# Attention stage of a decoder layer: one run of transpositions for each slot, with the compressed ones directly ahead of it and the preceding slot's first values ahead of both

## The chip, the cores and the metric

The kernel runs on one core of a Trainium2 chip. The metric is the time of one execution on the device, in microseconds (us); the median of three runs is given. One further execution was recorded by the hardware profiler, and all rows below come from it. The engines are TensorE (PE, with its weight loads listed apart as PEld), VectorE (DVE), ScalarE (ACT), GpSimd (POOL) and SyncE (SP), which issues DMAs.

## What is computed

One layer of a decoder trunk over 512 positions of width 2048, in float32. The part that matters here is the sparse attention: 16 heads of 64 in 4 groups, three branches (compressed, selected blocks, sliding window), each with its own keys and values, mixed by gates. Cut to that part, the reference is:

```python
q, kv, g_logits, z_a, uv, z_b, merge_logits = jnp.split(h @ w_in, SPLIT_IDX, axis=-1)
# compressed branch: 31 overlapping blocks of 32 positions
p_c = jax.nn.softmax(jnp.where(vc_mask, sc - slopes * dc, NEG), axis=-1) * vc_mask
o_c = jnp.einsum('bgrqn,bngd->bqgrd', p_c, vc)
# selected blocks and window: scores, ALiBi, softmax, values
p_s = jax.nn.softmax(ss);  o_s = jnp.einsum('bgrqnk,bgqnkd->bqgrd', p_s, vs)
p_w = jax.nn.softmax(sw);  o_w = jnp.einsum('bgrqk,bkgd->bqgrd', p_w, vwb)
o_a = (g0 * o_c + g1 * o_s + g2 * o_w) * silu(z_a)
```

Around it stand the input projection, a chunked gating branch, two up-projections, the output projection, a per-layer embedding under a gate and a final norm. With 512 positions there are 8 blocks of 64 and up to 16 may be selected, so the selected branch sees every causal position, as the window does.

## The kernel before

All matrix products with the large weights are done in two float32 parts, a high and a low one (`hi` and `lo`; three matmuls for each product). The halves are made by `split`: ScalarE casts the high part (`high`, line 200), VectorE subtracts to get the low one (`low`, line 206). With `later=True` the subtraction is put on the list `deferred`, and the next `flush` issues it.

Projections are a stream of small units of work, made by a generator. `fill(n)` takes the next n units from it; in the attention stage a unit is three matmuls of 512 columns (lines 588 to 590, tiles `ps_q` and `ps_za`), and their weight halves are made on ScalarE and VectorE two pieces ahead. These units are the filler between the pieces of attention, which are short and depend on each other.

The attention stage (trace: about 213 to 462 us) goes over 48 slots, six for each of eight feature tiles `ft` of two heads. A slot is a query tile `i` of 128 positions with one branch or both: `(ft, 3, (0,))`, `(ft, 3, (1,))`, `(ft, 2, (0,))`, `(ft, 2, (1,))`, `(ft, 1, (0, 1))`, `(ft, 0, (0, 1))`; `j` counts them from 0 to 5. The loop has 51 periods, and works on several slots at once: in period s it makes the `scores` of slot s (TensorE into `ps_s`, then a VectorE reduction, line 1611), the `exponentials` of s (ScalarE, line 1620), `weigh` of s - 1 (VectorE, line 1636), the transpositions of s - 2 (`transpose_probs`, line 1661) and the `values` of s - 3 (lines 1680 and 1681).

The transpositions of a slot come in one or two blocks of up to four. Each block fills one PSUM bank `ps_t` (there are two, of the kind "t"); ScalarE casts it to `pth`, VectorE makes `ptl` from both (three buffers of each), and `values` reads these two. For every even `ft` the compressed branch adds steps of its own: `cmp_softmax` at j = 1 (four transpositions into a bank of the kind "s", line 1733, a copy, a shift in three VectorE steps, lines 1743 to 1745), `cmp_weigh` at j = 3 (VectorE lines 1753 to 1755, then GpSimd lines 1756 and 1757), `cmp_transpose` at j = 4 (line 1763, then a copy `pc`, two casts and two subtractions). The banks of the kind "s" are shared by `ps_s` and `ps_c`, and there are two of them.

The order of a period is written out as the list `events`. After each event that uses TensorE some filler is taken by a running `credit`; `off_pe` events take none, and no event is followed by a `flush` of its own: the `flush` stands ahead of the next event that uses TensorE. In the list, the first block of transpositions stands ahead of the exponentials, the first block of values behind them, then `cmp_softmax` or `cmp_transpose`, then the second block of transpositions and the second block of values. All engines take their instructions in the order in which the program issues them.

Of the kernel before, what the change touches and what calls it, by code (L numbers as in the profile page):

```python
# [117 lines left out]
def kernel(ctx: ExitStack, tc: tile.TileContext, x, p, norm_g, w_in,  # L118
# [15 lines left out]
    def bank(kind, name):  # L134
        return psum.tile([P, 512], F32, tag=kind, name=name)
# [56 lines left out]
    def flush():  # L192
        todo = list(deferred)
        deferred.clear()
        for f in todo:
            f()
# [14 lines left out]
    def split(hi, lo, src, scale=None, later=False):  # L211

        high(hi, src, scale)
        if later:
            deferred.append(lambda: low(hi, lo, src, scale))
        else:
            low(hi, lo, src, scale)
# [120 lines left out]
    def load_next():  # L338
        while state["loads"] < len(loads):
            b = before[state["loads"]]  # L340
            tag = loads[state["loads"]][0]
            if tag in SPOTS and not spots.get(tag):
                return
            if b is not None and last_sub[b] >= state["low"]:
                return
            if tag not in SPOTS + ("raw",) and {"b11": "free"}.get(tag, "pool") not in quad:
                if not quad.get("b12"):
                    return
            load_to(state["loads"])
# [283 lines left out]
    def fill(n):  # L633
        for _ in range(n):
            next(run, None)
# [281 lines left out]
    phase_b_units = 16 * 14  # L917
# [721 lines left out]
    def blocks(s):  # L1639
        ft, i, br = slots[s]  # L1640
        if i == 0:
            return [[(0, 0), (1, 0)]]
        res = []
        for j in range(len(br)):
            ks = list(range(i + 1))
            for a in range(0, len(ks), 2):
                res.append([(j, k) for k in ks[a:a + 2]])
        return res
# [3 lines left out]
    def transpose_probs(s, bi):  # L1652
        ft, i, br = slots[s]
        n = (i + 1) * P
        pts = prob[s][0]
        bl = blocks(s)[bi]
        b = bank("t", "ps_t")
        for e, (j, k) in enumerate(bl):
            for hh in range(2):
                c = j * n + k * P  # L1660
                nc.tensor.transpose(b[:, (2 * e + hh) * P:(2 * e + hh + 1) * P], pts[hh][:, c:c + P], ident)  # L1661
        w = 256 * len(bl)
        hi = att.tile([P, S], F32R, tag="pth", name="pth", bufs=3)
        lo = att.tile([P, S], F32R, tag="ptl", name="ptl", bufs=3)
        split(hi[:, :w], lo[:, :w], b[:, :w], later=True)
        moved[s, bi] = (hi, lo)

    def values(s, bi):
        ft, i, br = slots[s]
        g = ft // 2  # L1670
        bl = blocks(s)
        hi, lo = moved.pop((s, bi))
        if i % 2 == 1 and br[0] == 0 and bi == 0:
            obank[ft, i // 2] = bank("o", "ps_o")
        o = obank[ft, i // 2][:, (i % 2) * 256:(i % 2) * 256 + 256]
        for e, (j, k) in enumerate(bl[bi]):
            w = vt[:, br[j], k, g]
            first = br[j] == 0 and bi == 0 and e == 0
            last = br[j] == 1 and bi == len(bl) - 1 and e == len(bl[bi]) - 1
            nc.tensor.matmul(o, w, hi[:, e * 256:e * 256 + 256], start=first, stop=False)  # L1680
            nc.tensor.matmul(o, w, lo[:, e * 256:e * 256 + 256], start=False, stop=last)
        if i % 2 == 0 and br[-1] == 1 and bi == len(bl) - 1:
            fold(ft, i // 2)

    def fold(ft, hf):
        o = obank.pop((ft, hf)).rearrange("p (i h q) -> p i h q", i=2, h=2)
        dst = o32[:, ft, 256 * hf:256 * hf + 256]
        gated = (ft, 256 * hf) in half_done
        tf = att.tile([P, S], F32, tag="zt", name="fold")[:, :256] if gated else dst
        half_done.add((ft, 256 * hf))  # L1690
        t = tf.rearrange("p (i q) -> p i q", i=2)
        nc.scalar.copy(t[0:64], o[64:128, :, 0])
        nc.scalar.copy(t[64:128], o[0:64, :, 1])

        def add():
            nc.vector.tensor_tensor(out=t[0:64], in0=t[0:64], in1=o[0:64, :, 0], op=ALU.add)
            nc.vector.tensor_tensor(out=t[64:128], in0=t[64:128], in1=o[64:128, :, 1], op=ALU.add)
            nc.gpsimd.tensor_tensor(out=tf, in0=tf, in1=oc_t[ft][:, 256 * hf:256 * hf + 256], op=ALU.add)
            if gated:
                nc.gpsimd.tensor_tensor(out=dst, in0=dst, in1=tf, op=ALU.mult)  # L1700
                o32_complete(ft, 1)
        deferred.append(add)
# [87 lines left out]
        f(0)  # L1790
    fill(6)
    n = len(slots)
    credit, per_period = 0.0, (phase_b_units - 19) / (n + 3)

    def load_sums(k):
        for p, o in (("5", ob_h), ("6", ob_l)):
            nc.gpsimd.dma_start(o[:, k], hsum_dram[p][:, k])

    for s in range(n + 3):
        events = []  # L1800
        state["slot"] = slots[s][0] if s < n else None, s % 6
        if s == n:
            quad["free"] = True
            load_next()
        if s < n:
            ft, j = slots[s][0], s % 6
            events.append((scores, s))
        if 1 <= s <= n:
            events.append((weigh, s - 1))
        if s < n and ft % 2 == 0 and j == 3:  # L1810
            events.append((cmp_weigh, ft // 2))
        tq = [(transpose_probs, s - 2, bi) for bi in range(len(blocks(s - 2)))] if 2 <= s <= n + 1 else []
        vq = [(values, s - 3, bi) for bi in range(len(blocks(s - 3)))] if s >= 3 else []
        more = s < n and ft % 2 == 1 and ft < 7 and j == 5
        if more:
            events.append((cmp_scores, (ft + 1) // 2, 0))
        events += tq[:1]
        if s < n:
            events.append((exponentials, s))
        events += vq[:1]  # L1820
        if more:
            events.append((cmp_scores, (ft + 1) // 2, 1))
        if s < n:
            if ft % 2 == 1 and ft < 7 and j == 3:
                events.append((cmp_keys, (ft + 1) // 2))
            if ft % 2 == 0 and (ft > 0 and j == 1 or j == 4):
                events.append(({1: cmp_softmax, 4: cmp_transpose}[j], ft // 2))
        if s in (0, 43):
            state.update(rate=0 if s else 1.41, due=0, late=0.6)
        if s in (26, 38):  # L1830
            load_sums(slice(0, 4) if s == 26 else slice(4, 6))
        events += tq[1:]
        if s < n and j == 5 - 2 * (ft % 2):
            events.append((cmp_values, ft))
        events += vq[1:]
        share = per_period / sum(e[0] not in off_pe for e in events)
        for at, e in enumerate(events):
            if e[0] not in off_pe:
                flush()
            e[0](*e[1:])  # L1840
            if e[0] not in off_pe:
                credit += share
                ahead = at + 1 < len(events) and events[at + 1][0] is cmp_transpose
                credit -= len(lent)
                lent.clear()
                units = max(int(credit) + ahead, e[0] is scores)
                fill(units)
                credit -= units
        if s % 6 == 5:
            for f in held:  # L1850
                f()
            held.clear()
# [584 lines left out]
    n = 0  # L2437
# [35 lines left out]
```

## Time and profile before

| | us |
|---|---|
| median of 3 runs | 1500.58 (1500.29 to 1500.77) |
| the profiled execution, whole | 1499.92 |
| its span, first to last instruction | 1498.2 |
| TensorE busy | 1488.6 (99%) |
| VectorE busy | 1238.9 (83%) |
| ScalarE busy | 879.3 (59%) |
| GpSimd busy | 434.6 (29%) |
| granted TensorE clock, mean | 0.999 |

An engine's busy time is a mean over stages. The starts of successive matmuls tell more than their durations, since matmuls overlap: a 512-column matmul is listed with 0.39 us, and the next one starts 0.23 us behind it. A wait shows as a start that is late against this step.

### The profile page before, as it was taken

To read this page: it belongs to the slowest core of one execution; us is meant where nothing else is said; L and a number is where in the kernel's file an instruction comes from. 1 tells how busy PE (TensorE), PEld (TensorE's weight loads), DVE (VectorE), ACT (ScalarE), POOL (GpSimd) and SP (SyncE) were. 2 spreads that over 40 slices of the span, in tenths; PEclk is the share of its full clock that TensorE was granted. 3 is DMA by queue.
4 is the path that set the end of the run, shared out by engine and by line. 5 is a ranking of instruction groups with operands and counts; after the bars stand their busy time and mean duration, and the time that the engine had idled before them with its cause. 6 is when DMAs were issued, how large, how long until landed. Compare 5 with 4: busy or idle time off the path is not lost.

```text
span 1498.2 us, 20471 instructions
## 1 busy us (share of the span) xinstructions
PE 1488.6 (99%) x7166; PEld 1245.0 (83%) x7166; DVE 1238.9 (83%) x1846; ACT 879.3 (59%) x1500; POOL 434.6 (29%) x650
## 2 busy tenths in 40 slices
PE   9999999999999999999999999999999999999998
PEld 8988888888888888888888888888888888888886
DVE  7887879999997888978888879797877985778877
ACT  7554467777765555555655555555556555655564
POOL 1331044333432242433444323221211223101220
PEclk9999999999999999999999999999999999999999
DMA  9789579889886795978798957596698999989693
GB/s 325 212 246 298 145 167 218 166 200 257 199 201 233 236 298 138 297 162 271 188 283 221 283 135 245 192 311 253 259 356 273 291 239 312 305 264 313 158 305 141
DMA packets 187063, 359.41 MB, mean 240 GB/s; under 512 B 15432, under 2 KB 73424, under 8 KB 184016
## 3 DMA queue, kind: packets, MB, share of 16 engines
q0 software_dynamic: 73472, 181.00, 46.1%
q1 hardware_dynamic: 113344, 176.84, 35.9%
q8 instruction: 56, 0.92, 0.2%
q14 instruction: 47, 0.39, 0.1%
q10 hardware_dynamic: 144, 0.26, 0.0%
HBM read 298.81 MB, written 114.82 MB: 276 GB/s over the span
## 4 chain that ended last, share of the span: by engine, by line
PE 92%; DVE 2%; issue 2%; DMA 1%; ACT 1%; POOL 1%; POOLq 0%; DVEq 0%; ACTq 0%
PE ps_m L561 6%; PE ps_m L562 6%; PE ps_m L563 6%; PE ps_wo L562 3%; PE ps_wo L563 3%; PE ps_wo L561 3%; PE ps_pg L500 3%; PE ps_pg L502 3%; PE ps_pg L501 3%; PE ps_t L1661 2%; PE ps_za L588 2%; PE ps_za L589 2%; PE ps_za L590 2%; PE ps_kv L561 2%; PE ps_u L561 2%
## 5 line engine op out<-in xcount | busy, mean ns | idle before, releaser
L206 DVE TENSOR_TENSOR ls<-b,hs 128x1024 fp32r<-128x1024 f32 x223 | 272.5, 1223 | 110.3 <-ACT hs L200 109.1
L200 ACT CAST hs<-b 128x1024 fp32r<-128x1024 f32 x223 | 234.7, 1053 | 203.2 <-PE ps_m L563 47.1
L200 ACT CAST hs<-raw 128x1024 fp32r<-128x1024 f32 x139 | 146.5, 1055 | 134.6 <-issue 34.3
L206 DVE TENSOR_TENSOR ls<-raw,hs 128x1024 fp32r<-128x1024 f32 x139 | 169.9, 1222 | 54.9 <-ACT hs L200 54.6
L464 POOL COPY pad_r<-pad_r 128x1 f32<-128x1 f32 x55 | 50.6, 920 | 211.7 <-ACT pad_r L463 211.6
L561 PE MATMUL ps_m<-hs,act_h 128*128 128x512 f32 x256 | 100.2, 391 | 0.0
L562 PE MATMUL ps_m<-ls,act_h 128*128 128x512 f32 x256 | 99.8, 390 | 0.0
L563 PE MATMUL ps_m<-hs,act_l 128*128 128x512 f32 x256 | 99.7, 389 | 0.0
L376 DVE TENSOR_TENSOR b<-raw,b 128x1024 f32<-128x1024 f32 x68 | 82.8, 1218 | 1.5 <-DMA raw<-in_w_in_dram 1.4
L376 DVE TENSOR_TENSOR b<-b,b 128x1024 f32<-128x1024 f32 x64 | 78.0, 1218 | 0.0
L200 ACT CAST pth<-ps_t 128x512 fp32r<-128x512 f32 (+1 forms) x88 | 47.6, 544 | 46.0 <-PE ps_t L1661 45.5
L1620 ACT ACTIVATE prob<-prob,st 128x512 f32<-128x512 f32 (+3 forms) x128 | 70.7, 556 | 5.3 <-DVE st L1611 5.2
L206 DVE TENSOR_TENSOR lo<-raw,hi 128x512 fp32r<-128x512 f32 (+1 forms) x96 | 63.2, 663 | 6.3 <-ACT hi L200 5.5
L200 ACT CAST hi<-raw 128x512 fp32r<-128x512 f32 (+1 forms) x96 | 56.1, 591 | 19.0 <-PE ps_vcg L603 5.3
L206 DVE TENSOR_TENSOR ptl<-ps_t,pth 128x512 fp32r<-128x512 f32 (+1 forms) x88 | 55.5, 636 | 8.0 <-ACT pth L200 7.3
L1611 DVE CUSTOM_DVE_ANT_0 prob<-ps_s,b 128x512 f32<-128x512 f32 (+3 forms) x128 | 56.1, 485 | 3.9 <-PE ps_s L1602 3.6
L562 PEld LDWEIGHTS ps_m<-ls,act_h 128*128 128x128 f32 x256 | 48.1, 188 | 10.3 <-DVE ls L206 0.5
L563 PEld LDWEIGHTS ps_m<-hs,act_l 128*128 128x128 f32 x256 | 48.1, 188 | 10.2
L561 PEld LDWEIGHTS ps_m<-hs,act_h 128*128 128x128 f32 x256 | 48.1, 188 | 9.8
L588 PE MATMUL ps_za<-act_h,hi 128*128 128x512 f32 x128 | 53.9, 421 | 0.0
L1636 DVE TENSOR_SCALAR prob<-prob,st,gates 128x512 f32<-128x512 f32 (+3 forms) x128 | 51.9, 458 | 1.8
L588 PE MATMUL ps_q<-act_h,hi 128*128 128x512 f32 x128 | 52.2, 407 | 0.0
(768 smaller groups left out, 4598.1 us busy)
## 6 DMA issues: line engine op xcount, KB each, us to landing
raw<-in_w_in_dram SPq DMA_DIRECT2D x112, 512.0 KB, 5.3
b<-in_w_in_dram SPq DMA_DIRECT2D x58, 512.0 KB, 6.5
o<-in_w_out_dram POOLq DMA_DIRECT2D x48, 512.0 KB, 7.8
t<-in_w_up_b_dram POOLq DMA_DIRECT2D x24, 512.0 KB, 9.6
b<-o SPq DMA_DIRECT2D x18, 512.0 KB, 7.3
o<-o POOLq DMA_DIRECT2D x16, 512.0 KB, 6.3
act_l<-gate POOLq DMA_DIRECT2D x8, 1024.0 KB, 12.7
g<-in_w_ple_gate_dram POOLq DMA_DIRECT2D x16, 512.0 KB, 7.6
```

Of the source, the lines that this page charges most:

```text
L200: nc.scalar.copy(hi, src)
L206: nc.vector.tensor_tensor(out=lo, in0=src, in1=hi.bitcast(F32), op=ALU.subtract)
L376: nc.vector.tensor_tensor(out=b[o], in0=b[x], in1=b[y], op=ALU.subtract)
L464: nc.gpsimd.tensor_copy(steps[:, 16 + i:17 + i], steps[:, i:i + 1])
L500: nc.tensor.matmul(o, ah, hi[:, i], start=begins, stop=False, skip_group_check=go)
L561: nc.tensor.matmul(o, ah, wh, start=st, stop=False, skip_group_check=go)
L562: nc.tensor.matmul(o, ah, wl, start=False, stop=False, skip_group_check=go)
L563: nc.tensor.matmul(o, al, wh, start=False, stop=sp, skip_group_check=go)
L588: nc.tensor.matmul(ps, hi[:, j], ah, start=st, stop=False)
L1611: nc.vector.tensor_tensor_reduce(out=pt[:, j * n:j * n + n], in0=o[:, j], in1=b0[:, 512 - n:], scale=-SLOPE[h], scalar=3.0e38, op0=ALU.add ...
L1620: nc.scalar.activation(sl, sl, AF.Exp, bias=st[:, 0, j, hh:hh + 1], scale=-1.0, accum_out=st[:, 1, j, hh:hh + 1])
L1636: nc.vector.tensor_scalar(out=sl, in0=sl, scalar1=st[:, 1, j, hh:hh + 1], scalar2=gates[:, i, gate:gate + 1], op0=ALU.mult, op1=ALU.mult)
```

## The change

The loop's list of events is put in another order. All blocks of transpositions of a slot are one event now (`transpose_all`), behind the first block of values of the preceding slot. `cmp_softmax` and `cmp_transpose` stand between these two, and no filler is taken behind them, so their four transpositions come directly ahead of the slot's own. The exponentials follow behind the transpositions. The count of units that the filler holds back goes from 19 to 20.

```diff
+    def transpose_all(s):
+        for bi in range(len(blocks(s))):
+            transpose_probs(s, bi)
+
...
-    credit, per_period = 0.0, (phase_b_units - 19) / (n + 3)
+    credit, per_period = 0.0, (phase_b_units - 20) / (n + 3)
...
-        tq = [(transpose_probs, s - 2, bi) for bi in range(len(blocks(s - 2)))] if 2 <= s <= n + 1 else []
+        tq = [(transpose_all, s - 2)] if 2 <= s <= n + 1 else []
         vq = [(values, s - 3, bi) for bi in range(len(blocks(s - 3)))] if s >= 3 else []
...
-        events += tq[:1]
+        events += vq[:1]
+        if s < n and ft % 2 == 0 and (ft > 0 and j == 1 or j == 4):
+            events.append(({1: cmp_softmax, 4: cmp_transpose}[j], ft // 2))
+        events += tq
         if s < n:
             events.append((exponentials, s))
-        events += vq[:1]
...
-            if ft % 2 == 0 and (ft > 0 and j == 1 or j == 4):
-                events.append(({1: cmp_softmax, 4: cmp_transpose}[j], ft // 2))
...
-        events += tq[1:]
...
+                if e[0] in (cmp_softmax, cmp_transpose):
+                    continue
                 units = max(int(credit) + ahead, e[0] is scores)
```

TensorE in the period of slot 16 (ft = 2, j = 4; about 286 to 291 us), from behind the scores to behind the compressed transpositions (`ps_c`), before:

```order
L1661 MATMUL ps_t<-ident,prob 128x128 x4
L1680 MATMUL ps_o<-pth,vt 128x256
L1681 MATMUL ps_o<-ptl,vt 128x256
L1680 MATMUL ps_o<-pth,vt 128x256
L1681 MATMUL ps_o<-ptl,vt 128x256
L588 MATMUL ps_q_3094<-act_h_90,hi 128x512
L589 MATMUL ps_q_3094<-act_l_91,hi 128x512
L590 MATMUL ps_q_3094<-act_h_90,lo 128x512
L588 MATMUL ps_q_3094<-act_h_90,hi 128x512
L589 MATMUL ps_q_3094<-act_l_91,hi 128x512
L590 MATMUL ps_q_3094<-act_h_90,lo 128x512
L1763 MATMUL ps_c<-ident,b_2793 128x128 x4
```

The two transpositions of the slot's second block follow there (`ps_t`, x2). The same place now:

```order
L1684 MATMUL ps_o<-pth,vt 128x256
L1685 MATMUL ps_o<-ptl,vt 128x256
L1684 MATMUL ps_o<-pth,vt 128x256
L1685 MATMUL ps_o<-ptl,vt 128x256
L588 MATMUL ps_q_3083<-act_h_90,hi 128x512
L589 MATMUL ps_q_3083<-act_l_91,hi 128x512
L590 MATMUL ps_q_3083<-act_h_90,lo 128x512
L1767 MATMUL ps_c<-ident,b_2793 128x128 x4
L1661 MATMUL ps_t<-ident,prob 128x128 x6
L588 MATMUL ps_q_3083<-act_h_90,hi 128x512
L589 MATMUL ps_q_3083<-act_l_91,hi 128x512
L590 MATMUL ps_q_3083<-act_h_90,lo 128x512
```

The values moved ahead of the slot's transpositions, these moved behind the compressed ones, and one filler unit less stands ahead of the compressed ones.

VectorE one period earlier (slot 15, j = 3; about 284 to 289 us), from the weighing on, before (`cst` is what GpSimd waits for, `lo` the filler's low half):

```order
L1636 TENSOR_SCALAR prob<-prob,st,gates 128x384 x2
L1753 TENSOR_REDUCE cst<-b_2793 128x16
L1754 RECIPROCAL cst<-cst 128x16
L1755 TENSOR_TENSOR cst<-cst,gates 128x16
L206 TENSOR_TENSOR ptl<-ps_t,pth 128x512
L206 TENSOR_TENSOR lo<-raw,hi 128x512
L206 TENSOR_TENSOR ptl<-ps_t,pth 128x512
```

And now:

```order
L1636 TENSOR_SCALAR prob<-prob,st,gates 128x384 x2
L1757 TENSOR_REDUCE cst<-b_2793 128x16
L1758 RECIPROCAL cst<-cst 128x16
L1759 TENSOR_TENSOR cst<-cst,gates 128x16
L206 TENSOR_TENSOR lo<-raw,hi 128x512
L206 TENSOR_TENSOR ptl<-ps_t,pth 128x512 x2
```

The first `ptl` moved behind the filler's `lo`, and stands directly ahead of the second.

ScalarE in the period of slot 16 again, before, with the exponentials of slot 16 (`prob`, x4):

```order
L200 CAST pth<-ps_t 128x512 x2
L1620 ACTIVATE prob,st<-prob,st 128x256 x4
L200 CAST hi<-raw 128x512
L1765 COPY pc<-ps_c 128x512
L200 CAST b_3178<-pc 64x512 x2
L200 CAST pth<-ps_t 128x256
```

And now:

```order
L1769 COPY pc<-ps_c 128x512
L200 CAST b_3162<-pc 64x512 x2
L200 CAST pth<-ps_t 128x512
L200 CAST pth<-ps_t 128x256
L1620 ACTIVATE prob,st<-prob,st 128x256 x4
```

The compressed copy and both casts of the slot's transpositions moved ahead of the exponentials.

## Rows read from the trace of the kernel before

**Rows 1.** The page: busy us of each engine (share of span), instructions.

```profile
PE 1488.6 (99%) x7166; PEld 1245.0 (83%) x7166; DVE 1238.9 (83%) x1846; ACT 879.3 (59%) x1500; POOL 434.6 (29%) x650
```

**Rows 2.** Windows: length; busy PE, PEld, DVE, ACT, POOL; clock, DMA share, GB/s.

```profile
213.00:462.00 249.00, 248.07 (x1432) 212.57 (x1431) 228.49 (x638) 178.75 (x474) 97.10 (x134) 1.00 0.86 205
267.00:295.00 28.00, 27.53 (x166) 23.50 (x165) 26.16 (x70) 20.27 (x52) 12.28 (x15) 1.00 0.72 165
```

**Rows 3.** Waits from 213 to 462 us: us in total, times, longest.

```profile
PE ps_t L1661 <- DVE ptl L206: 0.9, 2, 0.5
PEld ps_t L1661 <- DVE ptl L206: 3.6, 8, 0.9
ACT pth L200 <- PE ps_t L1661: 45.5, 30, 2.7
```

**Rows 4.** Timeline, TensorE: start us, us, engine, line, operation, out<-in, count.

```profile
309.13 0.60 PE L1661 MATMUL ps_t<-ident,prob 128*128 128x128 f32 x4
...
309.80 0.40 PE L589 MATMUL ps_za<-act_l,hi 128*128 128x512 f32 x1
310.03 0.40 PE L590 MATMUL ps_za<-act_h,lo 128*128 128x512 f32 x1
...
1129.64 0.39 PE L562 MATMUL ps_ub<-ls,ob_h 128*128 128x512 f32 x1
...
1133.26 0.39 PE L563 MATMUL ps_ub<-hs,ob_h 128*128 128x512 f32 x1
1133.49 1.03 PE L2205 MATMUL ps_m<-ident,act_h 128*128 128x128 f32 x8
...
1134.60 0.40 PE L562 MATMUL ps_ub<-ls,ob_h 128*128 128x512 f32 x1
```

**Rows 5.** Timeline, the period of slot 16, all engines; idle time in brackets.

```profile
286.37 0.68 DVE L206 TENSOR_TENSOR ptl<-ps_t,pth 128x512 fp32r<-128x512 f32 x1
286.63 1.05 POOL L1756 TENSOR_TENSOR b<-b,cst 128x512 f32<-128x512 f32 x1 [1.42 <-DVE cst L1755]
286.97 1.25 DVE L206 TENSOR_TENSOR lo<-raw,hi 128x512 fp32r<-128x512 f32 x1
287.75 0.79 POOL L1757 TENSOR_TENSOR b<-b,o 128x128 f32<-128x128 f32 x1
...
289.08 0.42 DVE L1611 CUSTOM_DVE_ANT_0 prob<-ps_s,b 128x256 f32<-128x256 f32 x1
...
289.65 0.63 PE L1763 MATMUL ps_c<-ident,b 128*128 128x128 f32 x4
...
293.65 0.86 ACT L200 CAST pth<-ps_t 128x256 fp32r<-128x256 f32 x2
...
294.06 0.40 PE L590 MATMUL ps_q<-act_h,lo 128*128 128x512 f32 x1
294.45 0.42 DVE L206 TENSOR_TENSOR ptl<-ps_t,pth 128x256 fp32r<-128x256 f32 x1
...
294.93 0.20 PEld L1661 LDWEIGHTS ps_t<-ident,prob 128*128 128x128 f32 x2 [0.91 <-DVE ptl L206]
294.93 0.44 PE L1661 MATMUL ps_t<-ident,prob 128*128 128x128 f32 x2 [0.47 <-DVE ptl L206]
```

**Rows 6.** Timeline, the period of slot 13 (ft = 2, j = 1), VectorE and TensorE.

```profile
271.90 0.69 DVE L1611 CUSTOM_DVE_ANT_0 prob<-ps_s,b 128x512 f32<-128x512 f32 x1
...
273.16 0.60 PE L1733 MATMUL ps_c<-ident,b 128*128 128x128 f32 x4
...
274.44 0.67 DVE L206 TENSOR_TENSOR ptl<-ps_t,pth 128x512 fp32r<-128x512 f32 x1
...
276.19 0.40 PE L588 MATMUL ps_q<-act_h,hi 128*128 128x512 f32 x1
276.35 0.69 DVE L1744 TENSOR_REDUCE cst<-b 128x16 f32<-128x512 f32 x1
...
277.07 0.69 DVE L1745 TENSOR_TENSOR b<-b,cst 128x512 f32<-128x512 f32 x1
```

## The prediction

> **What bounds the kernel now.** I read the page's busy shares first. TensorE is busy 99% of the span [rows 1], so time can only be gained by giving it less to do, or by closing the little holes in front of its matmuls, and it can only be lost by opening new holes. Then I cut the span at the attention stage, which is all that the change touches: in the 249 us from 213 to 462 TensorE is busy 248.07 us, VectorE 228.49 and ScalarE 178.75 [rows 2]. The stage is bound by TensorE, with VectorE close behind. In the narrower stretch from 267 to 295 us VectorE is busy 26.16 of 28 us, and TensorE only 27.53: here VectorE lags and TensorE waits for it. So the third view is the list of waits in the stage. TensorE and its weight loads wait there for almost one thing only, `ps_t` for `ptl`: 0.9 us in 2 waits of the matmuls, 3.6 us in 8 waits of the loads [rows 3]. That is the wait of a transposition for its PSUM bank: the two `ps_t` banks take turns, and a bank is free again once VectorE has made `ptl` out of it. The last view is the timeline around such a place.
>
> **The change, part one: runs of transpositions are joined.** By the order of instructions the stage has 92 unbroken runs of transpositions before and 49 now, so 43 starts and ends of a run fall away; the number of transpositions, matmuls, copies and subtractions stays the same, and no DMA is issued by a moved step itself. What does a start and an end cost? A run of four begins at 309.13, and the second matmul behind it at 309.80 [rows 4]. That is 0.67 us, of which 0.23 is the ordinary step of the 512-column matmul in between (309.80 to 310.03 is one), so the run costs 0.44, or 0.11 for each transposition. A run of eight stands outside the stage: from 1133.49 to the second matmul behind it at 1134.60 are 1.11 us, less 0.23 they are 0.88. Two runs of four and one run of eight cost the same to the hundredth: joining saves nothing that these rows show, with an error of about 0.01 us a run, 0.4 us in all. There is one finer sign. Behind the run of four the step is 0.23, while 16 steps in an undisturbed stretch take 3.62 us, 0.226 each (1129.64 to 1133.26). If the 0.004 are paid by about eight matmuls behind each run, 43 runs are worth 43 x 0.03 = 1.4 us. Bounds: 0 to 1.4; I take 0.5, nearer to the rows that compare runs directly.
>
> **Part two: the bank waits.** At 294.06 the last matmul ahead of a run starts, and the run only at 294.93, 0.87 later where 0.23 is ordinary: 0.64 us lost [rows 5]. The cause is readable: the bank was filled at about 290.1 directly behind the compressed transpositions of 289.65, ScalarE copied it only at 293.65, because the exponentials, the compressed copy and two casts stood ahead, and VectorE subtracted at 294.45. The changed order puts both `pth` copies ahead of the exponentials on ScalarE, and both `ptl` next to each other on VectorE, so a bank is emptied sooner after it is filled. The weight load in front of that run idled 0.91 us for 0.64 us of lost time, so 0.27 of such a wait is free; the eight waits of 3.6 us then cost 3.6 - 8 x 0.27 = 1.4 us. Bounds: 0.9 (what the matmuls themselves show) to 3.6. I take 1.4 as saved.
>
> **Part three: what is late next.** Three things now stand earlier on TensorE than what they depend on may allow. First the compressed transpositions, seven of them inside the loop. In the period of 286 us they came at 289.65, behind four transpositions (0.44) and behind one filler unit (three matmuls of 0.23, 0.69) that now both stand after them, so they will be reached 1.13 us sooner, at 288.52. They need an `s` bank that VectorE's reduction of this slot's first head frees. Its second half starts at 289.08 and ends at 289.50 [rows 5], so by VectorE's times of before 0.98 us would be waited; GpSimd's multiplications, which end at 288.54 (287.75 + 0.79), cost 0.02. Against it, VectorE should get there sooner: its `lo` at 286.97 took 1.25 us where `ptl` of the same size takes 0.68, because GpSimd's first multiplication ran from 286.63 to 287.68; `lo` now comes directly behind the step that releases GpSimd, 0.6 sooner, and should be through without that loss. In the period of 271 us the softmax transpositions came at 273.16 and are reached at 272.03, while the reduction of the first head ends at about 272.6 (271.90 + 0.69) [rows 6]: 0.57 us. TensorE's queue goes no further meanwhile: the slot's transpositions and the filler stand behind.
>
> Second, the first values of the preceding slot. They are moved ahead of the transpositions, so about one run and one filler unit (1.1 us) less lies between `ptl` and its reader. In the period of the softmax `ptl` also falls behind the three VectorE steps of the shift. By rows 6: weighing ends at 274.44 (start of `ptl` there), three shift steps of 0.72 end at 276.6, `ptl` of 0.6 at 277.2. The reader is due at 276.19 + 0.69 = 276.88, and later by the 0.57 just lost: 277.45. So here nothing is left to wait, or 0.3 us if the first wait does not come. Third, the exponentials stand behind a second `pth` copy, on an engine that itself idled 45.5 us in 30 waits for transpositions [rows 3]; the weighing that reads them comes a whole period later, so I cost this at nothing. If that cover goes, VectorE's weighing waits by one copy (0.6 us) in such a period.
>
> These waits do not add up: a hole at the period's softmax moves TensorE back against VectorE and gives slack to the next place. For the sum: seven compressed places between 0 and 1.13 us, so 0 to 7.9. Only about two of the even features have VectorE lagging as in the rows (the 267 to 295 stretch and its twin one quarter later), so I take two times 0.55, 1.1 us.
>
> The filler units are spread with 20 instead of 19 held back, over 51 periods: 4.00 a period for 4.02. No unit is lost; what is not filled in the loop is run right behind it. Cost nothing.
>
> **Sum.** -0.5 - 1.4 + 1.1 = -0.8 us. The profiled execution had 1499.92 us, 1498.2 of them span, so it would become 1499.1; the median of the runs is 1500.58, and the forecast goes by it: 1499.8 us.
>
> **A rule to weigh.** In rows 5 `lo`, which reads two tiles of SBUF, ends 0.54 us behind GpSimd's multiplication, just its own length: it seems to have stood still until 287.68. The Trainium skill, "SBUF — State Buffer", "Who interferes with whom", says so: a VectorE instruction with two inputs in SBUF and a GpSimd instruction that reads SBUF exclude each other, and the one that starts first keeps the port for its whole length. The trace agrees (1.25 for 0.6 to 0.7 us). The rule speaks against this change in one point: now `lo` starts first, and GpSimd has to stand still; what that gives is rival 3.
>
> **The rivals.**
> 1. No new wait appears, and the old ones go: -0.5 - 1.4 = -1.9, at the far bounds -1.4 - 3.6 = -5.0; I take 1498.2. For it: VectorE is ordered better. Against it: its 26.16 of 28 us do not get less. Chance 0.20, of which 0.05 lie beyond 0.2%.
> 2. Slower: the compressed transpositions wait for the `s` bank or for GpSimd at all seven places by the whole 1.13 us, 7.9 - 1.9 = +6.0: 1506.6. It decides on the slower side from 0.7 us a place (7 x 0.7 - 1.9 = 3.0). For it: the reduction ends at 289.50 against 288.52. Against it: the first and the last of the even features have VectorE less far behind. Chance 0.14.
> 3. GpSimd's multiplications get later. `lo` starts 0.6 sooner (at 286.37, in `ptl`'s old place) and runs to about 287.0, GpSimd starts behind it instead of at 286.63, and its end moves from 288.54 to about 288.9 [rows 5]. The compressed transpositions, due at 288.52, wait 0.4 us for it even if VectorE has freed the bank. With the same in the twin stretch that is 0.8 us; where the bank wait of the forecast (1.1) is shorter than I took, these come in its place, and where it is not, half of them come on top: -0.4, so 1500.2. Chance 0.20.
> 4. The forecast, -0.8: 0.46.
>
> **How the numbers follow.** 0.2% are 3.0 us, about what a measurement of this kernel can tell from no change. Faster beyond that: 0.05, from rival 1. Slower: 0.14, rival 2. Within: 0.81. The range takes rival 1 down to 1497.9 (2.7 saved) and the forecast with new waits of 3.9 us instead of 1.1 up to 1502.6; that leaves out rival 2 and the far end of rival 1.
>
> **What would show it.** Joined runs: two groups of four as one run of eight that costs 0.88; if the step behind a run is 0.226 instead of 0.23, the larger bound holds. Bank waits: `ps_t` waiting for `ptl` below 1 us in the loads' list instead of 3.6. New waits: `ps_c` waiting for VectorE's `st` or `prob`, or `ps_o` waiting for `ptl`, each about 0.5 us and only in the even features. I would be wrong if `ps_o` waited for `ptl` in most periods (51 x 0.1 would be 5 us), or if TensorE's busy time outside 213 to 462 us changed.

## The result and the profile after

The changed kernel takes 1511.94 us (median of four runs, 1510.41 to 1512.08) against 1500.67 us for the kernel before on the same chip: 1.0074 times as long, 95% interval 1.0062 to 1.0086. It is slower by 11 us where I had forecast 0.8 us faster, and it lies 9 us above the end of my range. The profiled execution of the changed kernel is the one of 1510.41 us, with a span of 1508.7.

One line of its page, the busy time of each engine, against [rows 1]:

```profile
PE 1490.5 (99%) x7166; PEld 1247.1 (83%) x7166; DVE 1241.2 (82%) x1846; ACT 879.8 (58%) x1500; POOL 436.2 (29%) x650
```

Every engine has as many instructions as before and nearly the same busy time. What was added is time in which TensorE stands still. The windows say where: of the changed kernel, up to the attention stage, the stage, and behind it (columns as in [rows 2]), and then the first and the last of the kernel before.

```profile
0.00:213.00 213.00, 211.16 (x1074) 180.39 (x1075) 171.43 (x269) 124.53 (x233) 53.14 (x99) 1.00 0.80 235
213.00:472.50 259.50, 250.08 (x1427) 214.38 (x1426) 230.01 (x637) 178.83 (x473) 99.39 (x134) 1.00 0.83 196
472.50:1508.70 1036.20, 1029.23 (x4669) 852.36 (x4667) 839.77 (x942) 576.43 (x794) 283.69 (x417) 1.00 0.82 250
```

```profile
0.00:213.00 213.00, 211.45 (x1073) 180.72 (x1074) 171.11 (x269) 124.16 (x233) 52.85 (x99) 1.00 0.80 235
462.00:1498.20 1036.20, 1029.13 (x4665) 851.72 (x4663) 839.35 (x941) 576.37 (x794) 284.69 (x417) 1.00 0.82 249
```

Ahead of the stage and behind it the two kernels agree to a few tenths of a us of work in the same time, at a granted clock of 1.00. The stage has grown from 249 us to 259.5, and TensorE's idle time in it from 0.93 us (249 - 248.07, [rows 2]) to 9.42. The list of waits from 213 to 480 us, matmuls and weight loads (us in total, times, longest), stands against [rows 3]:

```profile
PE ps_o L1685 <- DVE ptl L206: 3.7, 6, 1.1
PE ps_s L1601 <- ACT b L1722: 2.9, 3, 1.0
PE ps_c L1737 <- DVE st L1611: 2.7, 3, 0.9
PEld ps_o L1685 <- DVE ptl L206: 7.3, 12, 1.4
PEld ps_s L1601 <- ACT b L1722: 4.2, 3, 1.4
PEld ps_c L1737 <- DVE st L1611: 3.3, 3, 1.1
```

The old waits of `ps_t` are gone. Three new kinds are there, each at a place that comes back with the features. The two lists differ for the same holes (3.7 and 7.3 us for `ptl`), so I also added up how late matmuls start in the stage against the ordinary step (all starts that are more than 0.15 us late). Before, that is 1.6 us at 4 places, all `ps_t`. Now it is 12.0 us at 16 places: 5.3 for `ps_o`, 3.4 for `ps_s` and 3.4 for `ps_c` (3.2 of it at the three places in the list). The difference, 10.4 us, is nearly all of the 10.5 us by which the stage has grown. One of each from the timeline.

**Wait A**, the scores of the next slot for ScalarE's copy of the second compressed scores (`cmp_scores`, part 1), at the end of each odd feature but the last:

```profile
263.77 0.70 PE L1719 MATMUL ps_c<-b,kcp 128*128 128x512 f32 x2
263.89 0.86 ACT L200 CAST pth<-ps_t 128x512 fp32r<-128x512 f32 x2 [0.40 <-PE ps_t L1661]
...
265.80 0.40 ACT L1620 ACTIVATE prob<-prob,st 128x128 f32<-128x128 f32 x1
266.18 0.40 PE L590 MATMUL ps_q<-act_h,lo 128*128 128x512 f32 x1
266.30 0.58 ACT L1720 COPY b<-ps_c 64x512 f32<-64x512 f32 x1
266.89 0.58 ACT L1722 COPY b<-ps_c 64x512 f32<-64x512 f32 x1
267.52 0.50 PE L1601 MATMUL ps_s<-ob_h,b 128*128 128x512 f32 x1 [0.95 <-ACT b L1722]
267.87 0.40 PE L1602 MATMUL ps_s<-ob_l,b 128*128 128x512 f32 x1
```

From one matmul to the next are 1.34 us (266.18 to 267.52) where a step is 0.23, and the next step is 0.35: a hole of 1.23 us. On ScalarE the two copies of the compressed scores stand behind both `pth` casts and the slot's exponentials; the bank is free only when the second copy has been made. The kernel before had the same four exponentials ahead of these copies, and was just in time:

```profile
262.38 0.63 PE L1715 MATMUL ps_c<-b,kcp 128*128 128x512 f32 x2
...
264.99 0.58 ACT L1718 COPY b<-ps_c 64x512 f32<-64x512 f32 x1
...
265.83 0.39 PE L1601 MATMUL ps_s<-ob_h,b 128*128 128x512 f32 x1
```

There the second copy ended 3.19 us behind the start of the compressed scores, and the bank was asked for 3.45 us behind it. In the changed kernel the copy ends 3.70 us behind that start, since the exponentials now wait for both casts, and the bank is asked for after 2.64 us (263.77 to 266.41, where the next matmul was due), since a unit of filler and the second block's transpositions no longer stand between. So this wait has two halves: 0.51 us of a later copy and 0.81 us of an earlier reader, against 0.26 us that were to spare.

**Wait B**, the compressed softmax's transpositions for VectorE's reduction of the slot's scores:

```profile
271.62 0.74 ACT L1620 ACTIVATE prob<-prob,st 128x512 f32<-128x512 f32 x1
...
272.47 0.40 PE L1601 MATMUL ps_s<-ob_h,b 128*128 128x512 f32 x1
...
273.54 0.36 ACT L1697 COPY fold<-ps_o 64x256 f32<-64x256 f32 x1
274.00 0.41 DVE L1700 TENSOR_TENSOR fold<-fold,ps_o 64x256 f32<-64x256 f32 x1 [1.42 <-ACT fold L1697]
274.42 0.28 PE L1685 MATMUL ps_o<-ptl,vt 128*128 128x256 f32 x1
274.88 0.69 DVE L1611 CUSTOM_DVE_ANT_0 prob<-ps_s,b 128x512 f32<-128x512 f32 x1
275.63 0.66 PE L1737 MATMUL ps_c<-ident,b 128*128 128x128 f32 x4 [0.93 <-DVE st L1611]
```

VectorE wasn't busy when TensorE came to need it: it had stood still for 1.42 us in front of the fold's first addition, because ScalarE's two copies for the fold stand behind the exponentials, and the reductions stand behind the fold on VectorE.

**Wait C**, the preceding slot's first values for the low part of their probabilities. The changed kernel, VectorE and TensorE:

```profile
243.02 1.40 DVE L208 SCALAR_TENSOR_TENSOR b<-ps_q,b 64x512 fp32r<-64x512 f32 x2
244.44 0.69 DVE L206 TENSOR_TENSOR lo<-raw,hi 128x512 fp32r<-128x512 f32 x1
244.53 0.28 PE L1684 MATMUL ps_o<-pth,vt 128*128 128x256 f32 x1
245.17 0.69 DVE L206 TENSOR_TENSOR ptl<-ps_t,pth 128x512 fp32r<-128x512 f32 x1
245.91 0.39 PE L1685 MATMUL ps_o<-ptl,vt 128*128 128x256 f32 x1 [1.10 <-DVE ptl L206]
```

And VectorE in the same period of the kernel before:

```profile
242.62 1.39 DVE L208 SCALAR_TENSOR_TENSOR b<-ps_q,b 64x512 fp32r<-64x512 f32 x2
244.05 0.69 DVE L206 TENSOR_TENSOR ptl<-ps_t,pth 128x512 fp32r<-128x512 f32 x1
244.65 0.68 DVE L206 TENSOR_TENSOR lo<-raw,hi 128x512 fp32r<-128x512 f32 x1
```

Two things have met. The reader comes earlier, and `ptl` comes later: the transpositions are written behind a unit of filler now, and that unit's `lo` has slipped in front of `ptl` on VectorE.

### The profile page after: what moved, and what is told of

The parts are those of the page before. It is cut to its first block, busy times and chain, and to the rows that moved or that the text cites. A ratio compares the mean times of both kernels' runs of the same rounds, so it can differ in the third digit from the quotient of the medians.

```text
span 1508.7 us, 20489 instructions
## 1 busy us (share of the span) xinstructions
PE 1490.5 (99%) x7166; PEld 1247.1 (83%) x7166; DVE 1241.2 (82%) x1846; ACT 879.8 (58%) x1500; POOL 436.2 (29%) x650
## 4 chain that ended last, share of the span: by engine, by line
PE 89%; DVE 5%; ACT 3%; issue 2%; DMA 1%; POOL 0%; POOLq 0%; DVEq 0%; SPq 0%; ACTq 0%
PE ps_m L561 7%; PE ps_m L562 7%; PE ps_m L563 7%; PE ps_wo L561 3%; PE ps_wo L563 3%; PE ps_wo L562 3%; PE ps_pg L501 3%; PE ps_pg L500 3%; PE ps_pg L502 3%; PE ps_kv L561 2%; PE ps_kv L562 2%; PE ps_u L561 2%; PE ps_u L563 2%; PE ps_ua L562 2%; PE ps_ua L561 2%
## 5 line engine op out<-in xcount | busy, mean ns | idle before, releaser
L200 ACT CAST pth<-ps_t 128x512 fp32r<-128x512 f32 (+1 forms) x88 | 44.1, 549 | 30.4 <-PE ps_t L1661 30.1
```

What stands on the lines that cost most here:

```text
L200: nc.scalar.copy(hi, src)
```

## The experiments

The theory: the three waits are separate, each made by its own move, and together they are the whole loss. The rivals: one lagging engine (VectorE) is behind all of it, so that a cure at one place gives the time back at the next; or the filler's subtractions alone are to blame. Each difference below is against the kernel before on the same chip; the changed kernel itself stands at +11.3. The intervals are 3 to 5 us wide for most of the runs of the changed kernel, so differences of a us or two between such runs don't follow from these times; what sharpens them stands at the end of this section.

**Scores ahead.** The changed kernel, with the second compressed scores ahead of the joined transpositions:

```diff
         if more:
+            events.append((cmp_scores, (ft + 1) // 2, 1))
         events += tq
         if s < n:
             events.append((exponentials, s))
-        if more:
-            events.append((cmp_scores, (ft + 1) // 2, 1))
```

> The changed kernel, with the second compressed scores (cmp_scores, part 1) put ahead of the transpositions, so that their two ScalarE copies stand ahead of the slot's casts and exponentials. Theory of separate waits: TensorE's wait of ps_s for ScalarE's b (three times 1.12 us and three times 0.11 behind it in the changed kernel's trace) goes, 3.7 us less than the changed kernel, about 1508.2, and the other waits stay. Rival, VectorE's load: VectorE is too full in these stretches, and a hole closed in one place opens in the next; then less than 1.3 us are gained and the sum of the waits stays near 13.

Measured: 1507.90 us, +8.1, ratio 1.0053 [1.0036, 1.0070]. Wait A is gone from the list and the other two stand there unchanged (3.7 in 6 and 2.7 in 3).

**Softmax back.** The changed kernel, with the compressed softmax behind the exponentials and with filler behind it, as before; the compressed probabilities' transpositions (`cmp_transpose`) stay ahead:

```diff
-        if s < n and ft % 2 == 0 and (ft > 0 and j == 1 or j == 4):
-            events.append(({1: cmp_softmax, 4: cmp_transpose}[j], ft // 2))
+        if s < n and ft % 2 == 0 and j == 4:
+            events.append((cmp_transpose, ft // 2))
...
+            if ft % 2 == 0 and ft > 0 and j == 1:
+                events.append((cmp_softmax, ft // 2))
...
-                if e[0] in (cmp_softmax, cmp_transpose):
+                if e[0] is cmp_transpose:
```

> The changed kernel, with cmp_softmax (j = 1) alone back behind the exponentials and with filler behind it, as before the change; cmp_transpose stays ahead of the joined transpositions. Theory of separate waits: the wait of ps_c for VectorE's st (1.10, 1.04 and 1.04 us, and 0.06 each behind it) goes, 3.3 us less than the changed kernel, about 1508.6. Rival, VectorE's load: under 1.1 us gained, since the values of the next period then wait longer for ptl.

Measured: 1509.25 us, +9.4, ratio 1.0061 [1.0046, 1.0076]. Wait B is gone from the matmuls' list (0.6 us in 3 is left in the loads'), wait A is unchanged; the waits for `ptl` grew from 3.7 us in 6 to 4.5 in 7, so part of the gain went to the next place.

**Low parts at once.** The changed kernel, with `split(hi[:, :w], lo[:, :w], b[:, :w])` in `transpose_probs`, without `later=True`:

> The changed kernel, with ptl issued directly behind pth and not at the next flush, so that on VectorE it stands ahead of the filler's lo, the shift and the evacuation of the queries. Theory of separate waits: ps_o no longer waits for ptl (6.3 us in the changed kernel), 4 to 6 us less, about 1507. Rival, VectorE's load: VectorE's work is the same, so ps_o waits less, but lo, the shift or the reductions come later and the gain is under 2 us. A third possibility: ptl now makes VectorE stand still until ScalarE has made pth, and the kernel gets slower by up to 48 x 0.5 us.

Measured: 1511.99 us, +12.2, ratio 1.0082 [1.0067, 1.0097]. The edit left every engine's order as it was, so this is a second measurement of the changed kernel, on the chip of the runs around it. It excludes the putting off as the reason why `ptl` is late, and nothing more.

**Values behind.** The changed kernel, with the first values back behind the transpositions and the exponentials:

```diff
-        events += vq[:1]
         if s < n and ft % 2 == 0 and (ft > 0 and j == 1 or j == 4):
...
             events.append((exponentials, s))
+        events += vq[:1]
```

> The changed kernel, with the first values of the preceding slot back behind the transpositions and the exponentials; the joined run and the compressed transpositions ahead of it stay. Theory of separate waits: ps_o no longer waits for ptl (6.3 us less), but the compressed transpositions are reached another 0.5 to 1.1 us sooner, so the wait of ps_c for st grows by up to 3 x 1.1 us: 3 to 6 us less than the changed kernel, 1506 to 1509. Rival, VectorE's load: no gain beyond 1.5 us.

Measured: 1512.31 us, +12.5, ratio 1.0083 [1.0068, 1.0098]. No gain, where I had expected 3 to 6 us. TensorE's matmuls:

```profile
PE ps_c L1737 <- DVE st L1611: 5.0, 3, 1.7
PE ps_c L1767 <- DVE st L1611: 4.5, 4, 1.5
```

Wait C is gone altogether. But without the values and their unit of filler in front of them the compressed transpositions are reached 1.1 us sooner, and wait at all seven places.

**Scores and softmax.** The first two edits together:

> The changed kernel with both earlier edits at once: second compressed scores ahead of the transpositions, cmp_softmax back behind the exponentials. Alone they moved the changed kernel (1511.9) by -4.0 and -2.7 us. Theory of separate waits: the gains add, -6.7, about 1505.2, and what is left is ps_o waiting for ptl. Rival, one hole moves to the next place: not more than -4.5, and the waits for ptl grow by the rest.

Measured: 1506.29 us, +6.2, ratio 1.0039 [1.0025, 1.0054]. Only `ps_o` waiting for `ptl` is left in the matmuls' list, 4.4 us in 7. Against the second measurement of the changed kernel (+12.2) the two edits bring 4.1 and 2.7 us alone and 6.0 together; that the sum is 0.8 more is within the noise.

**Values alone.** The kernel before, with `events += vq[:1]` ahead of `tq[:1]` and 20 units held back:

> The kernel before, with one part of the change alone: the first values of the preceding slot ahead of the first block of transpositions (and 20 units held back instead of 19). The blocks stay apart and the compressed transpositions where they were. Theory of separate waits: this part brings the waits of ps_o for ptl, 3 to 6 us above the kernel before, 1503 to 1506, with no wait of ps_c for st and none of ps_s for b. Rival, the joined run brings them (ScalarE and VectorE get both blocks at once): within 1.5 us of the kernel before.

Measured: 1509.33 us, +9.2, ratio 1.0059 [1.0044, 1.0074]; I had expected half of that. `ps_o` waits for `ptl` (4.7 us in 6, longest 1.4), and `ps_t` too (1.1 in 4). So wait C comes with this move alone. Wait A hardly does (0.3 us in 1), and B does not.

**Joined alone.** The kernel before, with `tq = [(transpose_all, s - 2)]` and nothing else:

> The kernel before, with the other part alone: all transpositions of a slot in one run, at the place of the first block; values, compressed steps and filler rule as before. Theory of separate waits: the waits of ps_t for ptl go (2 us), ps_o does not wait for ptl, and ps_s may wait for the compressed scores' copy b, since the exponentials now stand behind two casts (0 to 3.3 us): 1498 to 1502. Rival, joining itself costs (two casts and two subtractions in a row): 1505 and more, with ps_o waiting for ptl.

Measured: 1503.86 us, +3.7, ratio 1.0023 [1.0012, 1.0035]. Its loads:

```profile
PEld ps_t L1661 <- DVE ptl L206: 4.0, 8, 0.8
PEld ps_s L1601 <- ACT b L1722: 1.9, 3, 0.8
```

The matmuls' list has 0.7 us in 2 of wait A, where the changed kernel has 2.9 in 3: joining brings a part of it, and the rest needs the values' move too. The bank waits of [rows 3] are about as long as before, only at other places (the longest at 310.79, 370.51 and 376.48 us instead of 294.93 and 359.63). By the order of the code a joined run needs its second bank sooner; no run shows that by itself.

**Joined, with the scores ahead.** The same, with the second compressed scores ahead of the run:

> As the run with joined transpositions alone, and the second compressed scores put ahead of the joined run. Theory of separate waits: no wait of ps_s for b, 1.5 to 2.5 us below the kernel before, about 1498. Rival, joining itself costs: above the kernel before by 3 us or more.

Measured: 1502.59 us, +2.5, ratio 1.0013 [1.0003, 1.0022]. The wait for ScalarE's copy is gone, the bank waits stay (1.3 in 3 and 3.9 in 8). What the remaining 2.5 us consist of these lists don't show.

**Compressed part alone.** The kernel before, with the compressed transpositions ahead of `tq[:1]`, 20 units held back:

```diff
+        if s < n and ft % 2 == 0 and (ft > 0 and j == 1 or j == 4):
+            events.append(({1: cmp_softmax, 4: cmp_transpose}[j], ft // 2))
         events += tq[:1]
```

> The kernel before, with the compressed part of the change alone: the compressed softmax's and the compressed probabilities' transpositions stand ahead of a slot's first transpositions, with filler behind them as before; transpositions in two runs, values where they were; 20 units of filler held back. Theory that each wait of the changed kernel belongs to its own move: TensorE's compressed transpositions wait for VectorE's reduction at three places by about 1 us (3 us in all, as with that move in the changed kernel), no waits of the values for their low parts, 1503 to 1504.5. Rival, that these waits come only where the first values stand ahead of them and pull everything earlier: below 0.5 us at each, 1500 to 1501.5. Rival, that the compressed transpositions wait still longer without the values' 1.1 us ahead of them (as with the values moved back in the changed kernel, 1.5 to 1.7 us at each of seven places): 1507 to 1511.

Measured: 1509.36 us, +8.9, ratio 1.0062 [1.0048, 1.0076]. The third expectation held, and so did what the run with the values moved back had shown: all seven places wait, the three of the softmax 0.8 to 1.2 us and the four of the compressed probabilities 1.5 to 1.9. VectorE and TensorE at the longest one:

```profile
289.59 0.69 DVE L206 TENSOR_TENSOR ptl<-ps_t,pth 128x512 fp32r<-128x512 f32 x1
290.19 1.25 DVE L206 TENSOR_TENSOR lo<-raw,hi 128x512 fp32r<-128x512 f32 x1
291.37 0.68 DVE L206 TENSOR_TENSOR ptl<-ps_t,pth 128x512 fp32r<-128x512 f32 x1
291.97 0.41 DVE L1611 CUSTOM_DVE_ANT_0 prob<-ps_s,b 128x256 f32<-128x256 f32 x1
...
292.88 0.63 PE L1763 MATMUL ps_c<-ident,b 128*128 128x128 f32 x4 [1.88 <-DVE st L1611]
```

Three subtractions stand ahead of the reductions, and TensorE, which has nothing between the slot's scores and the compressed transpositions but one unit of filler, waits for all of them.

**Exponentials later.** The kernel before, with the exponentials behind `tq[1:]` at the slots of `cmp_transpose`, against the old waits of [rows 5]:

> The kernel before, with one edit: at the slots at which the compressed probabilities are transposed (fourth fifth of an even feature) the slot's exponentials stand behind the slot's second transpositions instead of behind the first. TensorE's order is that of the kernel before. In the kernel before ScalarE does four exponentials (about 0.4 us each) between its copies of the first and of the second transposed probabilities, and copies that free PSUM banks stand behind them. Theory that copies standing behind exponentials are what TensorE waits for: some of the waits of TensorE's loads for ScalarE in these periods go, the next slot's weights come late by less than they have to spare, 1498.5 to 1499.7, ratio 0.999 to 1.0. Rival, that the exponentials are needed at once (the weighing on VectorE and the transpositions two slots later): new waits of about 0.5 us at seven places, 1502 to 1504.

Measured: 1500.81 us, +0.3, ratio 1.0 [0.9991, 1.0008]: no difference. The loads' waits of `ps_t` fell from 3.6 us in 8 to 1.8 in 5, and those of `ps_s` for ScalarE's copy `oc` rose from 0.4 in 2 to 2.3 in 4. The wait moved on to the next copy behind the exponentials.

**Low behind.** The changed kernel, with the look-ahead subtraction of the filler (`lo`) one unit later in the loop. That changes VectorE's order, and no other engine's:

```diff
-                split_to(si + state["ahead"] + (k if job.tail else 0), state["more"])
+                put_off = state["put_off"]
+                split_to(si + state["ahead"] + (k if job.tail else 0), state["more"], put_off < 0)
...
+                        if j == put_off:
+                            flush()
+                            split_to(si + state["ahead"], state["more"])
```

> The changed kernel, with one edit that alters VectorE's order alone: in the attention loop the filler's look-ahead subtraction (`lo`, 0.69 us) is issued one unit of filler later, so that at all places it stands behind `ptl` instead of ahead of it. TensorE, ScalarE, GpSimd and the transfers keep the order of the changed kernel. Theory that the first values wait for `ptl` because VectorE does `lo` ahead of it: ptl comes 0.69 us sooner in every such period, waits of 1.1 to 1.26 us shrink to 0.4 to 0.6 and the small ones go; of the 6.5 us some 4.5 are gained, 1507 to 1508.5; the waits for ScalarE's copy and for the reductions stay. Rival, that the reader is simply 1.1 us too early whatever stands ahead of `ptl` (it waits for ScalarE's `pth` and the weighing): unchanged, 1511 to 1512.5. Rival, that `lo` so late makes the filler's own matmuls wait: slower than the changed kernel, 1513 or more.

Measured: 1507.68 us, +7.5, ratio 1.0050 [1.0037, 1.0063], 3.8 us better than the changed kernel at +11.3 (4.7 against its second measurement). At the place shown above as wait C:

```profile
244.82 0.69 DVE L206 TENSOR_TENSOR ptl<-ps_t,pth 128x512 fp32r<-128x512 f32 x1
245.43 0.68 DVE L206 TENSOR_TENSOR lo<-raw,hi 128x512 fp32r<-128x512 f32 x1
245.56 0.39 PE L1689 MATMUL ps_o<-ptl,vt 128*128 128x256 f32 x1 [0.38 <-DVE ptl L206]
```

The wait is 0.38 instead of 1.10, shorter by the 0.7 of the one subtraction. In the whole stage the waits for `ptl` fell from 3.7 us in 6 to 0.8 in 3 (loads 7.3 in 12 to 2.0 in 4); A and B are unchanged.

**All three repairs.** The last edit with the first two:

> The changed kernel with three repairs together: the second compressed scores ahead of the joined transpositions, the compressed softmax back in its place of before, and `lo` behind `ptl` on VectorE. Theory of three separate waits: 1506.3 for the first two, less the 4.4 us of waits for `ptl` that were left with them, of which some 3 go: 1502 to 1503.5, the kernel before not reached. Rival, that without the three waits the shorter bank waits and joined runs show as a gain: 1499 to 1500. Rival, that VectorE is now behind everywhere and every gain at one place is lost at the next: 1505 to 1506.5.

Measured: 1502.13 us, +2.0, ratio 1.0013 [1.0004, 1.0022]. TensorE's matmuls, all that is left:

```profile
PE ps_c L1771 <- DVE st L1615: 0.9, 2, 0.6
PE ps_o L1689 <- DVE ptl L206: 0.8, 3, 0.4
```

The three repairs give back 9.3 of the 11.3 us (10.2 of the 12.2 of the second measurement, against which they gave 4.1, 2.7 and 4.7 alone, 11.5 added up).

The profiled executions say this more sharply. TensorE's last matmul of the loop's values, in the kernel before and in the changed kernel:

```profile
465.74 0.28 PE L1681 MATMUL ps_o<-ptl,vt 128*128 128x256 f32 x1
476.11 0.28 PE L1685 MATMUL ps_o<-ptl,vt 128*128 128x256 f32 x1
```

The same matmul starts at 476.16 us in the run with the low parts at once, which has the order of the changed kernel: two executions agree to 0.05 us up to here. Behind it the same two differ by 4 us, so in this pair the difference of the whole times arises behind the loop. Up to this matmul the runs compare so:

| | starts at, us | later than before, us |
|---|---|---|
| changed kernel | 476.11 | 10.4 |
| scores ahead (wait A away) | 472.52 | 6.8 |
| softmax back (wait B away) | 474.04 | 8.3 |
| values behind (wait C away, B longer) | 477.71 | 12.0 |
| low behind (most of wait C away) | 472.33 | 6.6 |
| scores and softmax | 470.31 | 4.6 |
| all three repairs | 466.39 | 0.6 |
| values alone | 474.65 | 8.9 |
| joined alone | 468.77 | 3.0 |
| joined, with the scores ahead | 467.20 | 1.5 |
| compressed part alone | 475.21 | 9.5 |

Alone the repairs bring 3.6, 2.1 and 3.8 us, 9.4 added up; together they bring 9.7. So to these repairs the waits are separate, and they are the loss: 9.7 of the 10.4 us. But they are not each made by a move of its own. The values alone make wait C, the compressed part alone makes B and four waits more, and A takes the joined run and the values' move together. No run beat the kernel before.

## Why the prediction was wrong

**What bounds the kernel** was read rightly: the loss is holes in front of TensorE's matmuls, inside the stage. What failed is part three, the price of the new holes: 1.1 us were forecast and 12.0 came.

**Part one, joining (0.5 saved).** The price of a run was right. In the changed kernel, TensorE's rows of a joined run:

```profile
269.97 1.04 PE L1661 MATMUL ps_t<-ident,prob 128*128 128x128 f32 x8
270.76 0.48 PE L588 MATMUL ps_q<-act_h,hi 128*128 128x512 f32 x1
271.08 0.40 PE L589 MATMUL ps_q<-act_l,hi 128*128 128x512 f32 x1
271.31 0.39 PE L590 MATMUL ps_q<-act_h,lo 128*128 128x512 f32 x1
```

From 269.97 to 271.08 are 1.11 us, less 0.23 they are 0.88, as forecast from [rows 4], and the step behind is 0.23: the larger bound is out. There was nothing to win here.

**Part two, bank waits (1.4 saved).** In the changed kernel they are gone, as said, and from start to start they had cost 1.6 us, near the 1.4 of the forecast. That is not the joining's doing: joined alone, they are 4.0 us in 8 against 3.6 in 8. That TensorE is held up elsewhere for 9 us, so that the banks have that long to come free, would be one reason, but it can't be all of it: with the three repairs most of that is gone, and no wait of `ps_t` came back. Why they went stays open.

**Part three, first step, compressed transpositions (1.1 lost).** That they are reached 1.13 us sooner was right for two of the three softmax places; at the third, around 410 us, it is 1.84. What failed is that I held them against VectorE's times of before. At the place of [rows 6] the softmax should wait 0.57 by those; its row says 0.93. The reduction there begins 1.94 us behind the slot's first scores (269.96 in the trace of before), in the changed kernel 2.41 (272.47 to 274.88), 0.47 later, and 0.57 and 0.47 make 1.04, where the hole measures 1.10 from start to start. At the other two places the reduction begins 0.16 and 0.36 later, and the holes are 1.04 each. The 0.47 come from the exponentials, below. The guess of two places was wrong too: three wait in the changed kernel's list, and all seven as soon as nothing stands ahead of them. Rival 2 had the mechanism and its direction, at more places than the whole change has.

**Second step, first values ("nothing left to wait, or 0.3").** This is the largest error: 7.3 us in 12 waits of the loads, 5.3 from start to start. I worked out one period, that of the softmax, and priced only the reader's 1.1 us. I had even seen the other half: I counted it a gain that `lo` comes 0.6 us sooner on VectorE, [rows 5], and did not ask what it overtakes. It overtakes `ptl`, and that puts the reader's own input 0.7 us back. The run with `lo` behind shows this half by itself: it is worth 3.8 us in the stage.

**Third step, exponentials ("I cost this at nothing").** The reader I named does come a period later. But ScalarE works in order, and I did not list what stands behind the exponentials on it: the copies of the compressed scores (about 0.5 us of each wait A, which is worth 3.6 us in the stage by the run that takes it away) and the fold's copies (0.47 us of the wait B shown above). In the kernel before the exponentials stood between two `pth` casts and could start while TensorE had not yet done the second block; behind both casts they start later, and so does all that stands behind them. The other half of wait A, the reader that comes 0.81 us sooner, is in no step of the prediction.

**The rivals.** Rival 1 fell with the waits. Rival 3 had the order of starts right, and not what it costs. In the period of slot 16 VectorE's `lo` now starts first, and GpSimd's first multiplication is held up:

```profile
289.36 0.68 DVE L206 TENSOR_TENSOR lo<-raw,hi 128x512 fp32r<-128x512 f32 x1
289.62 1.33 POOL L1760 TENSOR_TENSOR b<-b,cst 128x512 f32<-128x512 f32 x1 [2.02 <-DVE cst L1759]
```

`lo` takes 0.68 instead of 1.25, GpSimd's first multiplication 1.33 instead of 1.05 [rows 5]. The order of starts decides which of the two is delayed: at 424.75 us the multiplication starts first again and takes 1.05, and `lo`, at 425.10, takes 1.25. The Trainium skill, "SBUF — State Buffer", "Who interferes with whom", states it so, and the trace agrees. But the second multiplication (line 1761, at 291.04) takes 0.46 instead of 0.79, and the two together end 1.88 us behind GpSimd's start, where they ended 1.91 behind it before. So GpSimd doesn't get later by it. One load of the compressed transpositions, at 428.35, is listed with a wait of 0.5 us for GpSimd; that is in the period in which GpSimd had started first.

**Adding up.** The remark that the waits don't add up held for the moves and not for the repairs. The parts alone cost 3.7, 9.2 and 8.9 us, 21.8 together; all at once cost 11.3. One reason is shown: with the values back behind, the compressed transpositions wait 9.5 us at seven places by the matmuls' list, and with the values ahead of them 2.7 at three. That the rest is slack that one hole gives to the next is argued. I used this as a reason for a small sum. It limits the sum; it does not make it small. What I named as a sign against me, `ps_o` waiting for `ptl`, came, in 12 of the periods and not in most.

## What to carry to other kernels

When a step is moved in a loop whose engines work in order, write down for each engine what now stands in front of each result that another engine waits for, not only when its reader comes: here the reader came 1.1 us earlier and a subtraction of 0.7 us slipped ahead of its input. A long instruction on an engine that has idle time isn't free because its own reader is far off; the copies behind it that free banks pay. Where TensorE is busy 99% there is hardly anything to win by reordering, and every lead that is used up turns into a hole.

## What the runs showed of the hardware

A hole costs more than the idle time in its row. At 267.52 the row says 0.95 us, and the matmuls' starts lose 1.11 there (1.34 less 0.23); the matmul behind the wait runs 0.50 instead of 0.40, and its successor starts 0.12 us later than usual (0.35 for 0.23). Three such waits are 2.9 us in the matmuls' list and 4.2 in the loads', and were worth 3.6 us of the stage when they were taken away (476.11 to 472.52).
